# Hybrid encoder block on one core: last block's scans behind the first score tiles, gate steps spread over two heads, weight remainders off GpSimd, heads 4 to 7 first in the out projection

## Chip, cores and metric

The kernel runs on one core of a Trainium2 chip. The metric is the device time of one execution in microseconds (us). The engines are called by the profile's short names: PE (TensorE), DVE (VectorE), ACT (ScalarE), POOL (GpSimd), and SP (SyncE, which here only issues transfers).

## What is computed

One layer of an encoder with two branches beside each other. 1024 tokens and 16 meta tokens of width 1024 are normalized and projected once; the attention branch and the recurrent branch are gated, added, projected and added to the input; a second norm and a SwiGLU network of width 2816 follow, which the change does not touch.

```
proj = rmsnorm(h, norm1_g) @ w_in
q, k, v, xr, gr, g_merge = split(proj)
attn = bidirectional_gqa(rope(rmsnorm(q)), rope(rmsnorm(k)), v)     # 8 heads of 128, 2 key heads
xc   = centred_dwconv(xr)                                           # 4 taps
rnn  = (rg_lru(xc, ..., reverse=False) + rg_lru(xc, ..., reverse=True)) * gelu(gr)
g_attn, g_rnn = split(sigmoid(g_merge))
h = h + (g_attn * attn + g_rnn * rnn) @ w_out
h = h + swiglu(rmsnorm(h, norm2_g))

def rg_lru(xc, wa, ba, wx, bx, lam, reverse):
    r, i = sigmoid(xc @ wa + ba), sigmoid(xc @ wx + bx)             # 8 blocks of 128 channels
    a = exp(8 * r * log_sigmoid(lam))
    u = sqrt(1 - a * a) * (i * xc)
    h[t] = a[t] * h[t - 1] + u[t]                                   # or from the end
```

## The kernel before

A product in single precision is made of three matmuls: each operand is split into a rounded part and a remainder (`split`: ACT writes the rounded part with a Copy, line 100, another engine the remainder with a subtraction, line 102), and `mm3` adds hi·hi, hi·lo and lo·hi. The remainder is made on DVE, or on POOL where `split` is called with `G`.

The program has these stages, by the time of the profiled execution. Up to 488 us: norm and projections, and then a loop over the eight blocks `b` of the recurrent branch. For each block PE makes the products of the gate branch (`gm`, `gr`) and of the block's own gates (`gates`), `decays` makes the decays, and `scans` the square roots (ACT), the two scans and the result (DVE), which is stored as `rm_d[b]`. `tg` is the block's branch for the gelu. Behind the loop the first half of head 0's merge gate is made: the product `ga` on PE, then `gate`: a tanh on ACT (line 640) and one step on POOL. A tile scheduler lays out each engine's order from the order of the code, its priorities and the buffers; ACT has to load a table of functions when the kind of function changes.

From 488 to about 800 us: attention. It loops over heads `h` and over eight tiles `i` of 128 queries. The scores of a tile (27 matmuls into three banks, `S0` or `S1` by turns, `emit_scores`) are followed by the maximum on DVE (`nm`), the exponential on ACT (`p`), a scaled copy on ACT and its remainder on DVE (`PP`, two instructions, of 1024 and 16 columns) and a transposing transfer (`PT`). A scores buffer is free for the next tile but one when `p` is made. After every second tile the pair of tiles that lies two pairs back gets its product with v (`pv`, 25 matmuls, `emit_pv`), which DVE multiplies into the gate (`gar`). Between these, PE gets fill work in steps of 6 matmuls: the gate projection of the head after next (`ga_steps`, product `gap`), and in head 7 the out projection of heads 0 to 3 (`out_steps`, product `oph`, copied by DVE to `h`, line 804). `pv`, `gap` and `oph` share two "fill" banks by turns. How many fill steps follow a tile is set by hand:

```
            for _ in range(1 if h or i > 4 else 2 if i > 1 else 3):
                next(steps, None)
```

During heads 6 and 7 a table `ahead` sets by hand after which tile a load or a split of the out projection's operands stands: `M` (heads 0 to 3, loaded from DRAM; `M[c]` for each half c of the queries), `MH` (heads 4 to 7, head 4 loaded, the others straight from `gar`, function `keep`), and `wo` (eight pieces of the weights, `load_wout`; the remainder on POOL). A name in it means the next of two steps of that piece: load, then split.

From about 770 to 880 us: the rest of the out projection (`ops`, by `out_tile(t, n, kh)`: eight query tiles t, two column halves n, and kh = 0 for heads 0 to 3, that is `M`, kh = 1 for heads 4 to 7, that is `MH`), with the second norm of finished tiles and their transposes (`hT`) beside it. Then the network.

The functions that the change touches, with the line numbers of the profile:

Of the kernel before, what the change touches and what calls it, by code (L numbers as in the profile page):

```python
# [9 lines left out]
F32 = mybir.dt.float32  # L10
# [3 lines left out]
AF = mybir.ActivationFunctionType  # L14
ALU = mybir.AluOpType
# [5 lines left out]
T = 1024  # L21
NM = 16
NK = T + NM
HD = 128
NH = 8
NKV = 2
NB = 8
# [17 lines left out]
def tile_hybrid_encoder_block(  # L45
# [25 lines left out]
    V, S, G, PE, SP = nc.vector, nc.scalar, nc.gpsimd, nc.tensor, nc.sync  # L71
# [133 lines left out]
    def project(name, w, chunks):  # L205

        for c, a, e, o in chunks:
            ps = bank0(name)
            feat_project(ps[:, 0:e - a], w, c, a, e)
            yield ps[:, 0:e - a], o, e - a  # L210
# [305 lines left out]
    def load_gates(b):  # L516
        raw = pb.tile([128, 2, 2, 128], F32, name="graw")
        SP.dma_start(out=raw[:, :, 0], in_=rg_wa[0][:, b].rearrange("r c d -> c r d"))
        SP.dma_start(out=raw[:, :, 1], in_=rg_wx[0][:, b].rearrange("r c d -> c r d"))
        w = pb.tile([128, 2, 2, 2, 128], F32R, name="gw")  # L520
        split(raw, w[:, 0], w[:, 1])
        return w
# [50 lines left out]
                    S.activation(out=p[:, kind, a:e], in_=ps, func=AF.Sigmoid, bias=bias)  # L573
        return ri

    def decays(b, ri, xc):
        aa = page([128, 2, NK], F32, "aa")
        for r in range(2):
            p = ri[r]
            lo = 0 if r == 0 else NM  # L580
            rr, ii = p[:, 0, lo:NK], p[:, 1, lo:NK]
            a1, a2 = aa[:, r, lo:NK], pb.tile([128, NK], F32, name="a2")[:, lo:NK]
            cc = slice(8 * r + b, 8 * r + b + 1)
            S.activation(out=a1, in_=rr, func=AF.Exp, scale=ncL[:, cc])
            S.activation(out=a2, in_=a1, func=AF.Square)
            S.activation(out=rr, in_=rr, func=AF.Tanh, scale=cL[:, cc])

            V.scalar_tensor_tensor(out=rr, in0=a2, scalar=1.0, in1=rr, op0=ALU.add, op1=ALU.mult)
            V.tensor_tensor(out=ii, in0=ii, in1=xc[:, lo:NK], op=ALU.mult)
        return aa  # L590

    def scans(b, ri, aa, tg):
        for r in range(2):
            rr = ri[r][:, 0, (0 if r == 0 else NM):NK]
            S.activation(out=rr, in_=rr, func=AF.Sqrt)
        for r in range(2):
            p = ri[r]
            lo = 0 if r == 0 else NM
            rr, ii, a1 = p[:, 0, lo:NK], p[:, 1, lo:NK], aa[:, r, lo:NK]
            V.tensor_tensor(out=ii, in0=ii, in1=rr, op=ALU.mult)  # L600
            if r:
                rr, ii, a1 = rr[:, ::-1], ii[:, ::-1], a1[:, ::-1]
            V.tensor_tensor_scan(out=rr, data0=a1, data1=ii, initial=0.0, op0=ALU.mult, op1=ALU.add)
        hf, hb = ri[0][:, 0, NM:NK], ri[1][:, 0, NM:NK]
        V.tensor_tensor(out=hf, in0=hf, in1=hb, op=ALU.add)
        V.tensor_tensor(out=hf, in0=hf, in1=tg, op=ALU.mult)
        SP.dma_start(out=rm_d[b], in_=hf)

    def load_head(h, later=None):
# [6 lines left out]
            later.append(lambda: split(raw, q[:, 0], q[:, 1], G))  # L616
        return q

    gw = load_gates(0)
    conv = xr_project(0, xr0)  # L620
    for b in range(NB):
        sg = gm_project(b, next_block())
        tg = pb.tile([128, T], F32, name="tg")
        gr = gr_project(b, next_block(), sg, tg)
        next(gr)
        if b + 1 == NB:
            q = load_head(0)
        ri = gates(b, gw, conv[1])
        w = next_block()
        if b + 1 < NB:  # L630
            gw = load_gates(b + 1)
        next(gr)
        aa = decays(b, ri, conv[0])
        if b + 1 < NB:
            conv = xr_project(b + 1, project("xr", w, ALL))
        scans(b, ri, aa, tg)

    def gate(dst, ps):

        S.activation(out=dst, in_=ps, func=AF.Tanh, scale=0.5)  # L640
        G.tensor_scalar(out=dst, in0=dst, scalar1=1.0, scalar2=undo, op0=ALU.add, op1=ALU.mult)

    ga0 = page([128, 2, T], F32, "gar")
    SP.dma_start(out=ga0[:, 1], in_=rm_d[0])
    w_ga = next_block()

    for ps, o, n in project("ga", w, REAL[:1]):
        gate(ga0[:, 0, o:o + n], ps)

    p1b_pool.__exit__(None, None, None)  # L650
    psp.__exit__(None, None, None)
# [70 lines left out]
    def load_gar(h):  # L722
        g = page([128, 2, T], F32, "gar")
        SP.dma_start(out=g[:, 1], in_=rm_d[h])
        return g
# [19 lines left out]
    def behind():  # L745

        return copies[-3], maxima[-1]
# [26 lines left out]
    wo = {}  # L774

    def load_wout(j, n):

        raw = raw_tile([128, 2, 512])
        SP.dma_start(out=raw, in_=w_out[256 * j:256 * j + 256, 512 * n:512 * n + 512].rearrange("(k p) c -> p k c", p=128))
        wo[j, n] = page([128, 2, 2, 512], F32R, "wo")  # L780
        yield
        split(raw, wo[j, n][:, :, 0], wo[j, n][:, :, 1], G, behind=(copies[-3], None))
        yield


# [23 lines left out]
    def out_steps():  # L809
# [5 lines left out]
                yield from out_half(t, n, 0, fill_bank("oph"))  # L815

    pend = []
    gar = {0: ga0, 1: load_gar(1)}
    steps = chain(ga_steps(w, ga0, [1]), ga_steps(w_ga, gar[1]))

    items = {
        "M0": load_mix(0, 0), "M2": load_mix(0, 2), "M4": load_kept(4), "w00": load_wout(0, 0), "w10": load_wout(1, 0),
# [2 lines left out]
    }  # L825
    ahead = {
        (6, 1): ["M0", (5, 0)],
        (6, 2): ["M2"],
        (6, 3): ["M0", "w00"],
        (6, 4): ["w10"],  # L830
        (6, 5): ["M2", "w00", (5, 1)],
        (6, 6): ["w01"],
        (6, 7): ["w10", "M4"],
        (7, 0): ["w11"],
        (7, 1): ["w01", (6, 0)],
        (7, 3): ["M4", "w11", "w20"],
        (7, 5): [(6, 1)],
        (7, 6): ["w30"],
        (7, 7): ["w20", "w21", "w30", "w31", "w21", "w31"],
    }  # L840
    later = {}

    for h in range(NH):
        for i in range(8):
            emit_scores(h, i, q)
            for fn in later.pop((h, i), ()):
                fn()
            if i == (1 if h < NH - 2 else 0) and h + 1 < NH:
                q_n = load_head(h + 1, later.setdefault((h, i + 2), []))
            if i == 2 and h + 2 < NH:  # L850
                w_ga = load_block(COL_GA + 128 * (h + 2), G, later.setdefault((h, 4), []))
            if i == 3 and h + 2 < NH:
                gar[h + 2] = load_gar(h + 2)
            for nm in ahead.get((h, i), ()):
                if nm in items:
                    next(items[nm])
                else:
                    keep(*nm)
            if i == 5 and h + 2 < NH:
                steps = ga_steps(w_ga, gar[h + 2])  # L860
            if (h, i) == (NH - 1, 0):
                steps = out_steps()
            if i % 2 == 1:
                if len(pend) > 1:
                    u = pend.pop(0)
                    emit_pv(*u, gar[u[0]])
                pend.append((h, i // 2))
            for _ in range(1 if h or i > 4 else 2 if i > 1 else 3):
                next(steps, None)
        q = q_n  # L870
    for _ in steps:
# [48 lines left out]
    def norm2_rows(t):  # L920
        y = t4([128, D], F32, "y2")
        norm_rows(hres[t], 128, g2b, y)
        SP.dma_start(out=h_d[t], in_=hres[t])
        return y
# [68 lines left out]
    def out_tile(t, n, kh):  # L993
        for _ in out_half(t, n, kh, bank("ops")):
            pass
# [6 lines left out]
    for t in range(4):  # L1002
        xr[t] = raw_tile([128, D])
        SP.dma_start(out=xr[t], in_=x[128 * t:128 * t + 128])
        out_tile(t, 1, 1)
        V.tensor_tensor(out=hres[t], in0=hres[t], in1=xr[t], op=ALU.add)
        ys[t] = norm2_rows(t)
    for t in range(4, 8):
        out_tile(t, 0, 0)

# [146 lines left out]

    ww = {}  # L1160
    for t in range(4):
        out_tile(4 + t, 1, 0)
        norm2_lower(t, ys.pop(t))
        if t < 3:
            ww[4 + t] = wholes(4 + t)
# [5 lines left out]

    for t in range(4, 8):
        for n in range(2):
            out_tile(t, n, 1)
        ys[t] = norm2_rows(t)
        if t == 4:
            step_prep(0, 3)
        else:
            if t > 5:
                up(t - 2)  # L1180
            if t < 7:
                prep_early(t - 4)
# [170 lines left out]
```

## Time and profile before

| | |
|---|---|
| time of three runs | 1497.53, 1498.09, 1499.05 us; median 1498.09 |
| profiled execution | 1500.6 us, of which its span (first to last instruction) is 1498.7 us |
| mean granted clock of PE over the span | 0.995 of full speed |
| PE | busy 1472.1 us, 98% of the span, 7323 matmuls |
| DVE, ACT, POOL | busy 1116.7 us (75%), 744.6 us (50%), 249.2 us (17%) |

Times in the rows of a profile are counted from the start of the span. A row of the timeline gives start, length, engine, line, operation, output and inputs, and in brackets how long the engine had stood idle before it and what it waited for. An "x2" at the end means that neighbouring instructions of the same kind are drawn together, their lengths added.

### The profile page before, as it was taken

Reading aid. Unit: us, or ns where it says so; the run is one execution under the profiler, and the core shown is the slowest. Engines: PE = TensorE matmul, PEld = TensorE weight load, DVE = VectorE, ACT = ScalarE, POOL = GpSimd, SP = SyncE. Lnnn points to the kernel's source line nnn. Section 1 sums busy time; section 2 is a strip of 40 time slices with the busy share of each in tenths; the row PEclk is TensorE's granted clock in tenths of the full one; section 3 lists DMA queues with packets and bytes.
Section 4 is the critical chain, followed back from the end, with each engine's and each line's share of the span. In section 5 each row is a group of like instructions: output and inputs, shape, how many; then the busy total and the mean of one; then the engine's idle time right before and its main releaser. Section 6 shows DMA issues by size and latency. Waiting matters only on the chain. (4 is left out here: it accounts for less than half of the span.)

```text
span 1498.7 us, 20058 instructions
## 1 busy us (share of the span) xinstructions
PE 1472.1 (98%) x7323; PEld 1237.9 (83%) x7323; DVE 1116.7 (75%) x1707; ACT 744.6 (50%) x1244; POOL 249.2 (17%) x189
## 2 busy tenths in 40 slices
PE   7999999999999899999999999999999999999999
PEld 5888888888888788888877888888888888888887
DVE  6877666666776777777875799988888888747562
ACT  5544476667667666667752362322333332554330
POOL 0000000000000332222330201353433333200000
PEclk9999999999999999999999999999999999999999
DMA  7123212222212479896885334565564443898641
GB/s 247 53 73 101 85 35 64 64 64 63 64 57 71 131 190 206 200 202 159 191 187 185 96 100 140 161 189 191 181 199 161 162 160 115 290 333 282 218 144 59
DMA packets 300737, 219.98 MB, mean 147 GB/s; under 512 B 150648, under 2 KB 244304, under 8 KB 300640
## 3 DMA queue, kind: packets, MB, share of 16 engines
q1 hardware_dynamic: 300640, 218.72, 49.2%
q8 instruction: 57, 0.93, 0.3%
q14 instruction: 40, 0.33, 0.1%
HBM read 131.90 MB, written 51.12 MB: 122 GB/s over the span
## 5 line engine op out<-in xcount | busy, mean ns | idle before, releaser
L100 ACT ACTIVATE pw<-pr 128x1024 fp32r<-128x1024 f32 x77 | 80.3, 1062 | 105.6 <-PE po L1269 68.5
L100 ACT ACTIVATE wS<-s 128x512 fp32r<-128x512 f32 x88 | 53.3, 629 | 134.2 <-DVE s L1055 47.5
L1267 PE MATMUL po<-pw 128*128 128x512 f32 x308 | 119.8, 389 | 0.0
L1268 PE MATMUL po<-pw 128*128 128x512 f32 x308 | 119.8, 389 | 0.0
L1269 PE MATMUL po<-pw 128*128 128x512 f32 x308 | 119.8, 389 | 0.0
L102 DVE TENSOR_TENSOR pw<-pr,pw 128x1024 fp32r<-128x1024 f32 x77 | 92.5, 1241 | 34.9 <-ACT pw L100 28.7
L696 DVE SCALAR_TENSOR_TENSOR PP<-p,pr,PP 128x1024 f16<-128x1024 f32 (+1 forms) x128 | 106.6, 889 | 14.2 <-ACT PP L693 13.9
L687 ACT ACTIVATE p<-S,nm 128x1044 f32<-128x1044 f32 x64 | 72.4, 1131 | 65.5 <-DVE nm L684 55.2
L710 PE MATMUL pv<-PT,vt 128*128 128x256 f16 x800 | 94.6, 276 | 3.0 <-DVE h L804 3.0
L710 PEld LDWEIGHTS <-vt 128*128 128x128 f16 x800 | 76.5, 99 | 16.4 <-issue 3.6
L684 DVE TENSOR_REDUCE nm<-S 128x1 f32<-128x1044 f32 x64 | 78.2, 1236 | 9.2 <-PE S L109 9.0
L693 ACT ACTIVATE PP<-p,pr 128x1040 f16<-128x1040 f32 x64 | 73.9, 1154 | 5.3 <-issue 2.1
L102 DVE TENSOR_TENSOR wS<-s,wS 128x512 fp32r<-128x512 f32 x88 | 70.1, 815 | 0.0
L1267 PEld LDWEIGHTS po<-pw 128*128 128x128 f32 x308 | 57.8, 188 | 12.1
L1269 PEld LDWEIGHTS po<-pw 128*128 128x128 f32 x308 | 57.8, 188 | 12.0
L1268 PEld LDWEIGHTS po<-pw 128*128 128x128 f32 x308 | 57.8, 188 | 11.9
L1130 POOL TENSOR_TENSOR as<-act 128x512 f32<-128x512 f32 x11 | 16.6, 1508 | 305.4 <-DVE act L1118 254.1
L107 PE MATMUL S<-kT,qh 128*128 128x348 f32 (+1 forms) x192 | 62.3, 324 | 2.9 <-ACT p L687 2.9
L108 PE MATMUL S<-kT,qh 128*128 128x348 f32 (+1 forms) x192 | 62.0, 323 | 0.0
L109 PE MATMUL S<-kT,qh 128*128 128x348 f32 (+1 forms) x192 | 62.0, 323 | 0.0
L108 PE MATMUL xr<-xn,wblk 128*128 128x264 f32 (+1 forms) x192 | 61.4, 320 | 0.0
L109 PE MATMUL xr<-xn,wblk 128*128 128x264 f32 (+1 forms) x192 | 61.4, 320 | 0.0
(324 smaller groups left out, 4391.1 us busy)
## 6 DMA issues: line engine op xcount, KB each, us to landing
raw<-in_w_in_dram SPq DMA_DIRECT2D x44, 512.0 KB, 4.2
pr<-act_d SPq DMA_DIRECT2D x77, 256.0 KB, 5.2
raw<-in_w_ffn_in_dram SPq DMA_DIRECT2D x25, 512.0 KB, 4.7
wraw<-in_w_ffn_in_dram SPq DMA_DIRECT2D x22, 512.0 KB, 5.4
raw<-in_w_ffn_out_dram SPq DMA_DIRECT2D x22, 512.0 KB, 4.6
act_d<-as SPq DMA_DIRECT2D x44, 256.0 KB, 2.0
wot_d<-bs SPq DMA_DIRECT2D x44, 256.0 KB, 2.0
pr<-wot_d SPq DMA_DIRECT2D x44, 256.0 KB, 5.3
```

Source lines behind the costliest of these rows:

```text
L100: S.activation(out=hi, in_=src, func=AF.Copy)
L102: return (eng or V).tensor_tensor(out=lo, in0=src, in1=f32(hi), op=ALU.subtract)
L108: PE.matmul(out=ps, lhsT=lh, rhs=rl, start=False, stop=False)
L109: PE.matmul(out=ps, lhsT=ll, rhs=rh, start=False, stop=(k == n - 1))
L684: maxima.append(V.tensor_reduce(out=nm, in_=s[:, :, 0:KC], axis=AX.XY, op=ALU.max, negate=True))
L687: S.activation(out=p, in_=s[:, :, 0:KC], func=AF.Exp, bias=nm, accum_out=den)
L693: S.activation(out=pair[:, 0:NK], in_=pf, func=AF.Copy, scale=r)
L696: V.scalar_tensor_tensor(out=pair[:, o:o + e - a], in0=pf[:, a:e], scalar=r, in1=pair[:, a:e], op0=ALU.mult, op1=ALU.subtract)
L710: PE.matmul(out=ps, lhsT=vt[:, j, hl, vs], rhs=pt[:, m], start=(n == 0), stop=(n == len(terms) - 1))
L1267: PE.matmul(out=banks[t], lhsT=lh, rhs=w[:, 0, 1], start=j == 0, stop=False)
L1268: PE.matmul(out=banks[t], lhsT=lh, rhs=w[:, 1, 1], start=False, stop=False)
L1269: PE.matmul(out=banks[t], lhsT=ll, rhs=w[:, 0, 1], start=False, stop=j == NFP - 1)
```

## The change

Four things are changed. First, the last block's `scans` are taken out of the loop and called in attention behind the second score tile, with `tg` in a buffer of the raw ring, since the block's own buffers are gone by then; the roots get a function of their own, `roots`, and in the last block they are put behind the tanh of `ga`, which now belongs to the loop. Second, a set `rest` names four tiles in heads 5 to 7 that get no fill step, so that head 7's gate steps reach further into head 6, and `out_steps` starts one tile later. Third, the remainders of `wo` go from POOL to DVE, and the table `ahead` is written anew. Fourth, behind attention the products of heads 4 to 7 (kh = 1) come before those of heads 0 to 3 (kh = 0). PE makes the same matmuls, and ACT loads as many tables.

```diff
-    def scans(b, ri, aa, tg):
+    def roots(ri, behind=None):
         for r in range(2):
             rr = ri[r][:, 0, (0 if r == 0 else NM):NK]
-            S.activation(out=rr, in_=rr, func=AF.Sqrt)
+            with tc.issue_after(behind.ins) if behind else nullcontext():
+                S.activation(out=rr, in_=rr, func=AF.Sqrt)
+
+    def scans(b, ri, aa, tg):
...
-        tg = pb.tile([128, T], F32, name="tg")
+        tg = pb.tile([128, T], F32, name="tg") if b + 1 < NB else raw_tile([128, T])
...
+        th = None
+        if b + 1 == NB:
+            ga0 = page([128, 2, T], F32, "gar")
+            SP.dma_start(out=ga0[:, 1], in_=rm_d[0])
+            for ps, o, n in project("ga", w, REAL[:1]):
+                th = gate(ga0[:, 0, o:o + n], ps)
         if b + 1 < NB:
             conv = xr_project(b + 1, project("xr", w, ALL))
-        scans(b, ri, aa, tg)
+        roots(ri, th)
+        if b + 1 < NB:
+            scans(b, ri, aa, tg)
...
-        split(raw, wo[j, n][:, :, 0], wo[j, n][:, :, 1], G, behind=(copies[-3], None))
+        split(raw, wo[j, n][:, :, 0], wo[j, n][:, :, 1], behind=behind())
...
     ahead = {
         (6, 1): ["M0", (5, 0)],
...
+        (7, 5): ["w11", "w20"],
         (7, 6): ["w30"],
-        (7, 7): ["w20", "w21", "w30", "w31", "w21", "w31"],
+        (7, 7): ["M4", (5, 1), "w20", (6, 0), "w30", "w21", (6, 1), "w31", "w21", "w31"],
     }
+    rest = {(5, 6), (6, 0), (6, 2), (7, 0)}
...
+            if (h, i) == (0, 1):
+                scans(NB - 1, ri, aa, tg)
+                gar[1] = load_gar(1)
...
-            if (h, i) == (NH - 1, 0):
+            if (h, i) == (NH - 1, 1):
                 steps = out_steps()
...
-            for _ in range(1 if h or i > 4 else 2 if i > 1 else 3):
+            for _ in range(0 if (h, i) in rest else 1 if h or i > 4 else 2 if i > 1 else 3):
...
     for t in range(4, 8):
-        out_tile(t, 0, 0)
+        out_tile(t, 0, 1)
...
-        out_tile(4 + t, 1, 0)
+        out_tile(4 + t, 1, 1)
...
         for n in range(2):
-            out_tile(t, n, 1)
+            out_tile(t, n, 0)
```

On ACT, at the end of the last block (`ri` are the block's gates, `aa` and `a` its decays, `gar<-ga` the tanh of head 0's first gate half, which frees its bank), before:

```order
L584 ACT_TABLE_LOAD
L584 ACTIVATE aa<-ri,ncL 128x1024
L554 ACTIVATE tg<-tg 128x512
L585 ACTIVATE a_4381<-aa 128x1024
L586 ACTIVATE ri<-ri,cL 128x1024
L595 ACT_TABLE_LOAD
L595 ACTIVATE ri<-ri 128x1040
L595 ACTIVATE ri<-ri 128x1024
L640 ACT_TABLE_LOAD
L640 ACTIVATE gar<-ga 128x512
```

And the same place now (`raw` is now the name of `tg`):

```order
L585 ACTIVATE ri<-ri,cL 128x1040
L554 ACTIVATE raw<-raw 128x512
L583 ACT_TABLE_LOAD
L583 ACTIVATE aa<-ri,ncL 128x1024
L622 ACTIVATE gar<-ga 128x512
L584 ACTIVATE a_4381<-aa 128x1024
L585 ACTIVATE ri<-ri,cL 128x1024
L594 ACT_TABLE_LOAD
L594 ACTIVATE ri<-ri 128x1040
L594 ACTIVATE ri<-ri 128x1024
```

The tanh of `ga` has moved from behind the two roots to the place right behind the second exponential, ahead of a Square, a tanh, a table load and the roots.

On DVE, at the same time in the program (line 600 are the products ahead of the scans, 603 the scans, 605 and 606 the sum and the block's result, `nm` the maxima of the first score tiles), before:

```order
L600 TENSOR_TENSOR ri<-ri 128x1040
L600 TENSOR_TENSOR ri<-ri 128x1024
L603 SCALAR_TENSOR_TENSOR ri<-aa,ri 128x1040
L603 SCALAR_TENSOR_TENSOR ri<-aa,ri 128x1024
L605 TENSOR_TENSOR ri<-ri 128x1024
L606 TENSOR_TENSOR ri<-ri,tg 128x1024
L684 TENSOR_REDUCE nm<-S_4433 128x1
L689 TENSOR_SCALAR den<-den 128x1
L690 RECIPROCAL pr<-den 128x1
L696 SCALAR_TENSOR_TENSOR PP_4435<-p,pr,PP_4435 128x1024
```

And now:

```order
L604 SCALAR_TENSOR_TENSOR ri<-aa,ri 128x1040
L692 TENSOR_REDUCE nm<-S_4427 128x1
L697 TENSOR_SCALAR den<-den 128x1
L604 SCALAR_TENSOR_TENSOR ri<-aa,ri 128x1024
L698 RECIPROCAL pr<-den 128x1
L606 TENSOR_TENSOR ri<-ri 128x1024
L697 TENSOR_SCALAR den<-den 128x1
L607 TENSOR_TENSOR ri<-ri,raw 128x1024
L704 SCALAR_TENSOR_TENSOR PP_4428<-p,pr,PP_4428 128x1024
L704 SCALAR_TENSOR_TENSOR PP_4428<-p,pr,PP_4428 128x16
L698 RECIPROCAL pr<-den 128x1
L692 TENSOR_REDUCE nm<-S_4426 128x1
```

The maximum of the first tile stands ahead of this piece now, that of the second between the two scans, and the third tile's maximum comes behind the scans, the result and the first tile's PP.

On DVE, in the last pair of score tiles (tiles 6 and 7 of head 7; the product `gar<-gar,pv` frees a fill bank, COPY h<-oph another), before:

```order
L684 TENSOR_REDUCE nm<-S_4433 128x1
L684 TENSOR_REDUCE nm<-S_4434 128x1
L689 TENSOR_SCALAR den<-den 128x1
L690 RECIPROCAL pr<-den 128x1
L712 TENSOR_TENSOR gar<-gar,pv 128x256
L689 TENSOR_SCALAR den<-den 128x1
L690 RECIPROCAL pr<-den 128x1
L696 SCALAR_TENSOR_TENSOR PP_4437<-p,pr,PP_4437 128x1024
```

And now:

```order
L692 TENSOR_REDUCE nm<-S_4427 128x1
L102 TENSOR_TENSOR MH<-raw,MH 128x1024
L697 TENSOR_SCALAR den<-den 128x1
L102 TENSOR_TENSOR MH<-gar,MH 128x512
L698 RECIPROCAL pr<-den 128x1
L102 TENSOR_TENSOR wo<-raw,wo 128x2x512
L697 TENSOR_SCALAR den<-den 128x1
L720 TENSOR_TENSOR gar<-gar,pv 128x256
L704 SCALAR_TENSOR_TENSOR PP_4430<-p,pr,PP_4430 128x1024
L704 SCALAR_TENSOR_TENSOR PP_4430<-p,pr,PP_4430 128x16
L698 RECIPROCAL pr<-den 128x1
L102 TENSOR_TENSOR MH<-gar,MH 128x512
```

Two remainders of `MH` and one of `wo` now stand between the second maximum and the product that frees the bank, and more behind it; all eight remainders of `wo` stand on DVE from tile 7 of head 6 on.

## Rows read from the trace of the kernel before

**Rows 1.** The page: span, engine totals, and the exponential's group (busy, mean ns).

```profile
span 1498.7 us, 20058 instructions
...
PE 1472.1 (98%) x7323; PEld 1237.9 (83%) x7323; DVE 1116.7 (75%) x1707; ACT 744.6 (50%) x1244; POOL 249.2 (17%) x189
...
L687 ACT ACTIVATE p<-S,nm 128x1044 f32<-128x1044 f32 x64 | 72.4, 1131 | 65.5 <-DVE nm L684 55.2
```

**Rows 2.** Waits of PE by who ended them: total, times, longest.

```profile
PE gap L735 <- ACT gar L640: 4.4, 1, 4.4
PE pv L710 <- DVE h L804: 3.0, 1, 3.0
PE S L107 <- ACT p L687: 2.9, 1, 2.9
PE ops L800 <- DVE M L102: 2.5, 1, 2.5
...
PE xT L282 <- DVE ne L139: 0.6, 1, 0.6
```

**Rows 3.** Windows: length, busy PE, PEld, DVE, ACT, POOL, then granted clock, DMA.

```profile
18.00:26.00 8.00, 7.39 (x37) 5.90 (x36) 6.84 (x15) 5.25 (x12) 0.00 (x0) 1.00 1.03 408
...
487.00:500.50 13.50, 9.13 (x36) 6.87 (x34) 11.51 (x9) 7.90 (x9) 4.28 (x1) 0.87 0.09 23
724.00:738.00 14.00, 11.07 (x67) 9.90 (x65) 11.96 (x19) 9.69 (x16) 5.85 (x5) 0.88 0.78 194
762.00:772.00 10.00, 7.01 (x40) 5.45 (x40) 7.97 (x10) 7.44 (x11) 7.12 (x4) 0.83 0.80 185
811.00:823.00 12.00, 9.54 (x40) 7.47 (x39) 9.37 (x14) 3.09 (x7) 0.00 (x0) 0.86 0.59 186
```

**Rows 4.** Timeline of ACT at the end of the last block.

```profile
485.45 1.15 ACT L584 ACTIVATE aa<-ri,ncL 128x1024 f32<-128x1024 f32 x1
...
487.02 1.05 ACT L585 ACTIVATE a<-aa 128x1024 f32<-128x1024 f32 x1
...
493.75 0.60 ACT L640 ACTIVATE gar<-ga 128x512 f32<-128x512 f32 x1
```

**Rows 5.** Timeline of DVE, start of attention: the scans and the block's result.

```profile
493.82 4.50 DVE L603 TENSOR_TENSOR_SCAN ri<-aa,ri 128x1040 f32<-128x1040 f32 x2
...
499.84 1.23 DVE L606 TENSOR_TENSOR ri<-ri,tg 128x1024 f32<-128x1024 f32 x1
```

**Rows 6.** Timeline of PE: first matmuls of score tiles, a fill, the last wait.

```profile
514.72 0.32 PE L107 MATMUL S<-kT,qh 128*128 128x348 f32 x1
...
742.91 0.32 PE L107 MATMUL S<-kT,qh 128*128 128x348 f32 x1
...
744.33 0.48 PE L798 MATMUL oph<-wo,M 128*128 128x512 f32 x1
...
745.81 0.32 PE L107 MATMUL S<-kT,qh 128*128 128x348 f32 x1
...
751.37 0.32 PE L107 MATMUL S<-kT,qh 128*128 128x348 f32 x1
...
817.53 0.50 PE L800 MATMUL ops<-wo,M 128*128 128x512 f32 x1 [2.46 <-DVE M L102]
```

**Rows 7.** Timeline of DVE, head 7 and the out projection.

```profile
745.61 2.77 DVE L696 SCALAR_TENSOR_TENSOR PP<-p,pr,PP 128x1024 f16<-128x1024 f32 x4
...
756.90 2.39 DVE L684 TENSOR_REDUCE nm<-S 128x1 f32<-128x1044 f32 x2
...
761.69 4.98 DVE L696 SCALAR_TENSOR_TENSOR PP<-p,pr,PP 128x1024 f16<-128x1024 f32 x4 [0.50 <-ACT PP L693]
766.60 0.68 DVE L804 COPY h<-oph 128x512 f32<-128x512 f32 x1
...
816.25 2.36 DVE L102 TENSOR_TENSOR M<-raw,M 128x1024 fp32r<-128x1024 f32 x2
```

**Rows 8.** Timeline of POOL, end of head 7.

```profile
764.14 7.11 POOL L102 TENSOR_TENSOR wo<-raw,wo 128x1024 fp32r<-128x1024 f32 x3 [2.14 <-ACT wo L100]
```

More of the change, by code (lines that the diff above doesn't have):

```diff
@@ L574, in gates, with decays @@
         return ri
-    def decays(b, ri, xc):
-        aa = page([128, 2, NK], F32, "aa")
+    def decays(b, ri, aa, xc):
         for r in range(2):
@@ L589, in decays @@
             V.tensor_tensor(out=ii, in0=ii, in1=xc[:, lo:NK], op=ALU.mult)
-        return aa
-    def scans(b, ri, aa, tg):
+    def roots(ri, behind=None):
         for r in range(2):
             rr = ri[r][:, 0, (0 if r == 0 else NM):NK]
-            S.activation(out=rr, in_=rr, func=AF.Sqrt)
+            with tc.issue_after(behind.ins) if behind else nullcontext():
+                S.activation(out=rr, in_=rr, func=AF.Sqrt)
+    def scans(b, ri, aa, tg):
         for r in range(2):
@@ L617, in load_head, with gate @@
         return q
+    def gate(dst, ps):
+        th = S.activation(out=dst, in_=ps, func=AF.Tanh, scale=0.5)
+        G.tensor_scalar(out=dst, in0=dst, scalar1=1.0, scalar2=undo, op0=ALU.add, op1=ALU.mult)
+        return th
     gw = load_gates(0)
@@ L632, in tile_hybrid_encoder_block @@
         next(gr)
-        aa = decays(b, ri, conv[0])
+        aa = page([128, 2, NK], F32, "aa")
+        decays(b, ri, aa, conv[0])
+        th = None
[4 more added lines that the diff above has]
+                th = gate(ga0[:, 0, o:o + n], ps)
         if b + 1 < NB:
             conv = xr_project(b + 1, project("xr", w, ALL))
-        scans(b, ri, aa, tg)
[L638 to L644, printed above, removed]
+        roots(ri, th)
+        if b + 1 < NB:
+            scans(b, ri, aa, tg)
     w_ga = next_block()
-    for ps, o, n in project("ga", w, REAL[:1]):
-        gate(ga0[:, 0, o:o + n], ps)
     p1b_pool.__exit__(None, None, None)
@@ L817, in tile_hybrid_encoder_block, with second_gate @@
     pend = []
-    gar = {0: ga0, 1: load_gar(1)}
-    steps = chain(ga_steps(w, ga0, [1]), ga_steps(w_ga, gar[1]))
+    gar = {0: ga0}
+    def second_gate():
+        yield from ga_steps(w_ga, gar[1])
+    steps = chain(ga_steps(w, ga0, [1]), second_gate())
     items = {
@@ L827, in tile_hybrid_encoder_block @@
         (6, 1): ["M0", (5, 0)],
[L828 to L837, printed above, removed]
+        (6, 3): ["M0", "M2"],
+        (6, 5): ["M2", "w00"],
+        (6, 6): ["w10"],
+        (6, 7): ["w00", "w01"],
+        (7, 1): ["w10", "w11"],
+        (7, 3): ["w01", "M4"],
+        (7, 5): ["w11", "w20"],
         (7, 6): ["w30"],
-        (7, 7): ["w20", "w21", "w30", "w31", "w21", "w31"],
+        (7, 7): ["M4", (5, 1), "w20", (6, 0), "w30", "w21", (6, 1), "w31", "w21", "w31"],
     }
+    rest = {(5, 6), (6, 0), (6, 2), (7, 0)}
     later = {}
```

## The prediction

> **What bounds the kernel now.** I read the page first: the span is 1498.7 us and TensorE (PE) is busy for 1472.1 of it, 98% [rows 1]. The change alters no matmul, so it can only move time that PE spends waiting, or time at a lower clock. The waits of PE say where that is: behind the first loads, which the change doesn't touch, four waits stand out, 4.4, 3.0, 2.9 and 2.5, and the others are like the 0.6 shown with them [rows 2]. The windows around the four show the second half of their price: in each the mean granted clock is down, 0.87, 0.88, 0.83 and 0.86, because after the wait PE runs on the lower level (1.2 GHz) for some 3.4 us before it is back on 2.4 GHz [rows 3]. I count for each place the idle time plus (1 − clock) times the window:
>
> - A, start of attention: 4.37 + 0.13 × 13.5 = 6.1
> - B, before the score tiles of head 7: 2.93 + 0.12 × 14.0 = 4.6
> - C, end of head 7: 2.99 + 0.17 × 10.0 = 4.7
> - D, out projection: 2.46 + 0.14 × 12.0 = 4.1
>
> Together 19.5 us are all that this change can win, and 1498.1 − 19.5 = 1478.6 is the floor. The profiled execution took 1500.6, 0.17% above the median of the runs, and its span is 1.9 less; differences worked out inside the span I take off the median, 1498.1.
>
> **A, the scans.** PE's first gate step waits for a bank that ScalarE's tanh of `ga` frees, and this tanh runs at 493.75, behind a Square at 487.02, a tanh, two table loads and two roots [rows 4]. It ends at 494.35, so PE, which waited 4.4, got there at about 490.0 [rows 2, 4]. In the changed order the tanh stands right behind the exponential that ended at 485.45 + 1.15 = 486.60 before [rows 4]; a Square and a tanh of 1040 columns (about 1.1 each) and a tanh of 512 (0.6) now stand ahead of that exponential, so it ends near 489.4 and the tanh of `ga` near 490.0. The wait becomes 0 to 0.3: taken as 0.
>
> What is late next: the Square, the roots, and so the scans start 3.1 later (490.1 for 487.02). On VectorE (DVE) the chain of products, scans and the last multiplication ended at 499.84 + 1.23 = 501.07 [rows 5]; now it ends at 504.2, and with the second tile's maximum (1.2) between the scans at 505.4. Behind it stand PP of the first tile (1.4), two small steps (0.3) and the maximum of the third tile (1.2), to 508.3; its exponential takes 1.13 [rows 1], to 509.4. The fifth tile's scores need that buffer. PE started them at 514.72 [rows 6] and would come 6.1 sooner, at 508.6. So a new wait appears, 0.8 by this sum; if GpSimd, whose gate step took place beside the scans, makes these DVE steps some tenths slower it is up to 2.3. I take 1.2. A gains 6.1 − 1.2 = 4.9. On SP's queue the store of the eighth block's result and the loads of three gate rows now stand ahead of the first transposes; the store is ready at about 505, before the first PP (506.8), so it holds up none. The gate tile `tg` takes one of the three raw buffers until the scans end, so the first head's q is loaded some blocks' steps later, but still in the eighth block, with its split done before 488: cost 0, its cover being the block's own gate and projection steps.
>
> **B and C, head 6 to head 7.** Both come from DVE falling behind; at C the bank that PE's pv waits for comes free with the copy at 766.60, right behind four PP instructions. The four PP of a pair of tiles take 2.77 at 745.61, but 4.98 at 761.69, where GpSimd works on three `wo` remainders in 7.11 at 764.14 [rows 7, 8]: 2.2 more, while the split of the same size on DVE costs 2.36 / 2 = 1.18 [rows 7]. So a remainder costs DVE 1.0 less if DVE does it itself, where the two would overlap; where they wouldn't, it costs 1.2 more. The Trainium skill, "Perfetto Trace Analysis", Optimizing Scalar/DVE Operations, advises to take work off a saturated DVE, and warns that between DVE and GpSimd, which share a port, this might not help. The advice speaks against this change, the warning for it; by the advice alone eight remainders would only add 8 × 1.2 to DVE and the time would go towards that of the slower rival below.
>
> The second half is the gate steps. A pair of score tiles with two fills takes PE 751.37 − 742.91 = 8.46; one fill is 745.81 − 744.33 = 1.48, so with one 6.98, with none 5.50 [rows 6]. Before, three tiles had none between head 6 and 7; now four pairs have one each and the others two. DVE's time for a pair: from the maxima to PP 761.69 − 756.90 = 4.79 with a small split in it, plus 2.77, is 7.6 [rows 7]; a split of 1024 columns in the place of the small one makes it 7.7 to 7.8, a copy of an `oph` bank (0.68) besides 8.3 to 8.4. So DVE loses 0.6 to 1.1 in each pair with one fill, and regains up to 0.7 in one with two. I walked through the changed order from 692 with these times. The maxima of the pairs start on DVE at 710.1 (tile 2 of head 6), 718.2, 725.9, 733.7 (tile 0 of head 7), 741.4 and 749.7, the first tile's exponential ends 2.4 later (1.23 + 1.13), and PE wants the buffer at 713.0, 721.4, 729.7, 736.6, 744.9 and 753.3. It has 0.6, 0.8, 1.4, 0.5, 1.1 and 1.2 to spare: no wait at B.
>
> At the end it runs out. In the last pair DVE now does two MH splits and a `wo` split before the product that frees a `pv` bank: the second maximum ends at 760.9, then 1.2 + 0.7 + 1.2 + 0.4 and small steps, to 764.4, where PE wants the bank for an out-projection step at 763.0: 1.4. The step after next needs the copy of the bank before, behind two PP pairs and three more splits, 0.8 late. So of B and C, 9.3, I expect 2.2 to come back: gain 7.1.
>
> **Price of the new waits.** Does the clock drop after a wait of 0.8 to 1.4? No row here has one of that length. The wait of 0.6 near the start left the clock at 1.00 [rows 2, 3]; that of 2.46 was followed by 0.86 × 12 us [rows 3]. Both ends stay for the range: 0 or 1.7 for each. I take 0, as 1.2 and 1.4 are nearer to 0.6.
>
> **D, the order of the out projection.** PE waited until 817.53 for M of the second half, whose two splits (816.25, 2.36) stand on DVE behind norm2's work [rows 7]. Of the 108 matmuls of heads 4 to 7, whose inputs have long been split, the changed order puts all ahead of it, where before 48 were; the 60 more take 60 × 1.48 / 6 = 14.8 [rows 6], so M is wanted at 817.53 − 2.46 + 14.8 = 829.9 at the earliest, and even at their present place the splits end at 816.25 + 2.36 = 818.6. The cover is 11 us; without it the old wait would be back. Norm2's chain for the transposes between these products stays where it is on DVE and ScalarE. Gain 4.1.
>
> **Sum.** 4.9 + 7.1 + 4.1 = 16.1, and 1498.1 − 16.1 = **1482.0 us**.
>
> **The rivals.**
> - *DVE runs out sooner at the end.* A pair that costs DVE 0.2 more than worked out (the splits may take longer beside the products on GpSimd) adds 1.4 at the end: the wait of 1.4 becomes 2.8, over the 2.46 that did bring the lower clock, so 1.4 + 1.7 on top: 1485.
> - *The scans hold up the first tiles.* With DVE 1.3 later than worked out the wait at the fifth tile is 2.5 and the clock drops: 1.3 + 1.7 on top, again 1485. Both together give 1488.
> - *The stalls only move.* DVE's total work isn't less, and PE has no slack of its own: waits of the old size come back in other pairs. Then 1498. Against it: with GpSimd quiet there DVE's own pairs shrink by 2.2 where it collided, and the gate steps do fill the gaps.
> - *Slower: DVE becomes the bound.* From tile 7 of head 6 on eight remainders are added to DVE; PE's windows show it busy for 11.96 of 14 us just there [rows 3]. This decides if a remainder costs over 1.18 + 16.1/8 = 3.2 us each; at 3.8 it gives 1498 + 5 = 1503. The Trainium skill's page named above has the rule for it. Nothing on DVE of that shape takes over 1.2 while GpSimd is quiet.
> - *No new wait at all*: 1478.6.
>
> **How the numbers follow.** Chances: forecast 0.48 (own range 1480 to 1484); end sooner 0.18; first tiles 0.12; both 0.07; no new wait 0.06; stalls only move 0.05; slower 0.04. The range 1478 to 1489, from the floor to a little over both mishaps together, holds these but the last two, 0.91 by this count; I keep it that wide because the price of the clock drop rests on two rows. A measurement can tell 0.2%, 3 us. Faster 0.91, same 0.05, slower 0.04.
>
> **What would show it.** In the waits of PE the four of before should be gone: none on `gap` by the tanh of `ga`, none on `ops` by M; in their place one on S by `p` near 508 and one or two on `oph` near 763, each 0.7 to 1.5. The four PP of a pair should stay near 2.8 to head 7's end, and 128x1024 `wo` splits on DVE near 1.2. I am wrong if a wait of over 2 us stands anywhere behind 480, or if the granted clock drops in a place that had none.

## The result

| | before | after |
|---|---|---|
| median of the timed runs | 1497.81 us (1497.34 to 1499.05, 4 runs) | 1487.9 us (1487.38 to 1488.4, 4 runs) |
| ratio after / before, 95% interval | | 0.993 (0.9918 to 0.9942) |
| span of the profiled execution | 1498.7 us | 1486.6 us |
| mean granted clock over the span | 0.995 | 0.999 |

The change makes the kernel faster by 0.7%, 9.9 us of the forecast 16.1; the time lies in the range (1478 to 1489), near its upper end. The page after, span and engines:

```profile
span 1486.6 us, 20069 instructions
...
PE 1466.1 (99%) x7323; PEld 1233.6 (83%) x7323; DVE 1114.4 (75%) x1715; ACT 744.6 (50%) x1244; POOL 225.8 (15%) x181
```

The waits of PE after, by who ended them (total, times, longest), where [rows 2] had 4.4, 3.0, 2.9 and 2.5:

```profile
PE S L107 <- ACT p L695: 2.4, 1, 2.4
PE oph L806 <- DVE gar L720: 1.5, 1, 1.5
PE oph L806 <- DVE h L812: 0.9, 1, 0.9
PE gap L743 <- ACT gar L622: 0.6, 1, 0.6
...
PE pv L718 <- DMA PT<-PP: 0.4, 1, 0.4
```

All four old waits are gone or short, and the new ones stand where the forecast put them: one on S by `p`, two on `oph` by the `gar` product and by the copy. The two at the end have the size forecast (1.5 and 0.9 for 1.4 and 0.8); that on S has twice its size, 2.4 for 1.2, and there are two small ones, 0.6 and 0.4, that I had put at nothing. The windows of [rows 3] after, and one more around the new wait (length, busy PE, PEld, DVE, ACT, POOL, granted clock, DMA):

```profile
487.00:500.50 13.50, 12.90 (x62) 10.41 (x61) 10.67 (x11) 11.60 (x14) 2.32 (x6) 1.00 0.11 36
505.00:520.00 15.00, 12.59 (x63) 10.88 (x62) 12.79 (x18) 10.06 (x15) 5.81 (x5) 0.89 0.81 215
724.00:738.00 14.00, 14.00 (x98) 12.32 (x97) 12.57 (x22) 10.24 (x16) 2.32 (x3) 1.00 0.87 200
762.00:772.00 10.00, 7.66 (x32) 5.68 (x32) 10.00 (x16) 6.09 (x10) 1.72 (x1) 1.00 0.82 187
811.00:823.00 12.00, 12.00 (x63) 10.12 (x62) 10.29 (x19) 5.18 (x10) 1.29 (x1) 1.00 0.80 255
```

The clock is at 1.00 in all four old places, with waits of 1.5 and 0.9 in the fourth row; only around the wait of 2.4 it is down, 0.89. The timeline of DVE after shows why that wait is so long; the row of POOL under it stands beside the first:

```profile
502.62 1.23 DVE L606 TENSOR_TENSOR ri<-ri 128x1024 f32<-128x1024 f32 x1
...
503.88 3.42 DVE L607 TENSOR_TENSOR ri<-ri,raw 128x1024 f32<-128x1024 f32 x1
507.23 1.42 DVE L704 SCALAR_TENSOR_TENSOR PP<-p,pr,PP 128x1024 f16<-128x1024 f32 x2
...
508.65 1.22 DVE L692 TENSOR_REDUCE nm<-S 128x1 f32<-128x1044 f32 x1
...
503.82 2.41 POOL L102 TENSOR_TENSOR qh<-raw,qh 128x1024 fp32r<-128x1024 f32 x1 [4.13 <-ACT qh L100]
```

The last step of the scans takes 3.42 where it took 1.23 [rows 5], while GpSimd makes the remainder of head 1's q for 2.41. That pushes the maximum of the third tile from the forecast 507.1 to 508.7, and PE stands still until its exponential is done. In the trace of before the same remainder ran at 501.03, beside one maximum and a DVE that stood idle behind it (DVE, then POOL):

```profile
500.98 1.24 DVE L684 TENSOR_REDUCE nm<-S 128x1 f32<-128x1044 f32 x1
...
501.03 2.40 POOL L102 TENSOR_TENSOR qh<-raw,qh 128x1024 fp32r<-128x1024 f32 x1 [2.29 <-ACT qh L100]
```

At the other end of attention the forecast's steps can be read one by one from DVE's timeline:

```profile
727.54 1.22 DVE L102 TENSOR_TENSOR wo<-raw,wo 128x1024 fp32r<-128x1024 f32 x1
...
754.90 2.89 DVE L704 SCALAR_TENSOR_TENSOR PP<-p,pr,PP 128x1024 f16<-128x1024 f32 x4 [0.50 <-ACT PP L701]
...
762.48 1.20 DVE L102 TENSOR_TENSOR wo<-raw,wo 128x1024 fp32r<-128x1024 f32 x1
763.60 0.14 DVE L697 TENSOR_SCALAR den<-den 128x1 f32<-128x1 f32 x1
763.67 0.40 DVE L720 TENSOR_TENSOR gar<-gar,pv 128x256 f32<-128x256 f32 x1
```

A remainder of `wo` takes 1.2 on DVE, the four PP of a pair 2.9 where they took 4.98 [rows 7], and the product that frees the bank ends at 764.1 (forecast 764.4).

### The profile page after: what moved, and what is told of

It reads as the page before. It is cut to its first block, busy times and chain, and to the rows that moved or that the text cites. A ratio compares the mean times of both kernels' runs of the same rounds, so it can differ in the third digit from the quotient of the medians.

```text
span 1486.6 us, 20069 instructions
## 1 busy us (share of the span) xinstructions
PE 1466.1 (99%) x7323; PEld 1233.6 (83%) x7323; DVE 1114.4 (75%) x1715; ACT 744.6 (50%) x1244; POOL 225.8 (15%) x181
## 4 chain that ended last, share of the span: by engine, by line
PE 48%; DVE 3%; issue 1%; ACT 1%; ACTq 0%; DVEq 0%
PE po L1285 5%; PE po L1284 5%; PE po L1283 5%; PE A11B L1085 1%; PE A11B L1086 1%; PE A12B L1085 1%; PE S3T L1085 1%; PE S4B L1085 1%; PE A22T L1085 1%; PE S1T L1085 1%; PE S2T L1085 1%; PE S4B L1086 1%; PE A22T L1086 1%; PE S1T L1086 1%; PE S2T L1086 1%; PE S3T L1086 1%
## 5 line engine op out<-in xcount | busy, mean ns | idle before, releaser
L704 DVE SCALAR_TENSOR_TENSOR PP<-p,pr,PP 128x1024 f16<-128x1024 f32 (+1 forms) x128 | 98.2, 824 | 14.1 <-ACT PP L701 14.1
L1284 PEld LDWEIGHTS po<-pw 128*128 128x128 f32 x308 | 57.8, 188 | 12.1
```

The lines of the kernel that those rows point to most:

```text
L704: V.scalar_tensor_tensor(out=pair[:, o:o + e - a], in0=pf[:, a:e], scalar=r, in1=pair[:, a:e], op0=ALU.mult, op1=ALU.subtract)
L1284: PE.matmul(out=banks[t], lhsT=lh, rhs=w[:, 1, 1], start=False, stop=False)
```

## The experiments

My theory after the result: B and C went as forecast; the missing 6 us are the collision at the first tiles with what follows from it, and a profiled execution of before that had more clock drops than most. The rivals: the scans' chain is too long by itself, or another part of the change brought less than I think. The kernel before, timed beside these runs, has medians of 1497.8 to 1499.1, so a difference of about 1 us between two kernels that were not timed side by side says little.

### What each part is worth

**The scans where they were.** The changed kernel with the scans and the tanh of `ga` back at the end of the last block:

```diff
-        tg = pb.tile([128, T], F32, name="tg") if b + 1 < NB else raw_tile([128, T])
+        tg = pb.tile([128, T], F32, name="tg")
...
-            if (h, i) == (0, 1):
-                scans(NB - 1, ri, aa, tg)
```

> The changed kernel without its first part: the scans stand at the end of the last block again, tanh of ga behind the roots. Theory: the old wait of 4.4 with its clock drop (6.1 together) comes back, but the new ones (0.6, 2.42 with a drop of 1.65, 0.4, together 5.1) go: 1487.9 + 1.0 = 1489, so the first part bought about 1. Rival (the first part bought the 4.9 that was forecast and the loss is elsewhere): 1492.8.

Measured: 1489.66 us (1489.31 to 1489.74), ratio to before 0.9941 (0.9928 to 0.9953). The first part of the change is worth 1489.66 − 1487.9 = 1.8 by these times; against the kernel before as it was timed beside each, 1498.65 here and 1497.81 with the changed kernel, the two are 9.0 and 9.9 less, which makes it 0.9. Neither is near 4.9. The waits of PE in this run: the old one is back, and S and PT have none over 0.2.

```profile
PE gap L735 <- ACT gar L640: 4.4, 1, 4.4
PE oph L798 <- DVE gar L712: 1.5, 1, 1.5
PE oph L798 <- DVE h L804: 0.9, 1, 0.9
```

**The remainders of `wo` on GpSimd again.**

```diff
-        split(raw, wo[j, n][:, :, 0], wo[j, n][:, :, 1], behind=behind())
+        split(raw, wo[j, n][:, :, 0], wo[j, n][:, :, 1], G, behind=(copies[-3], None))
```

> The changed kernel with the eight remainders of wo on GpSimd again, everything else as changed. Theory (collisions on DVE decide): PP x4 of the pairs from tile 7 of head 6 take 4 to 5 in place of 2.8, DVE falls behind by 1 per pair, and PE waits 2 to 3 at the end of head 7 or before, with a clock drop: 1490 to 1493. Rival (spreading the gate steps did it, the place of the remainders is the same either way): 1488.

Measured: 1496.18 us (1494.47 to 1498.12), 8.3 slower than the changed kernel, more than the theory's 2 to 5. The rows of DVE and POOL show the collision:

```profile
737.73 4.97 DVE L704 SCALAR_TENSOR_TENSOR PP<-p,pr,PP 128x1024 f16<-128x1024 f32 x4 [0.50 <-ACT PP L701]
...
748.01 5.09 DVE L704 SCALAR_TENSOR_TENSOR PP<-p,pr,PP 128x1024 f16<-128x1024 f32 x4 [0.38 <-ACT PP L701]
...
740.18 2.50 POOL L102 TENSOR_TENSOR wo<-raw,wo 128x1024 fp32r<-128x1024 f32 x1 [2.13 <-ACT wo L100]
...
750.46 2.62 POOL L102 TENSOR_TENSOR wo<-raw,wo 128x1024 fp32r<-128x1024 f32 x1 [2.01 <-ACT wo L100]
```

Each remainder beside PP makes the four of them 5.0 instead of 2.8, and PE gets three waits of 1.7, 1.8 and 2.4 on `oph`. Behind the wait of 2.4, near 769, the clock falls (0.86 over 764 to 776). This profiled execution is the fastest of the ten, 1.7 under their median; where the others lose that is not seen in it. In all ten the time is 2.3 to 2.6 over the span, where the executions of the other kernels have 1.7 to 1.9, so some 0.7 of the 8.3 lies outside the first to the last instruction; why stays open.

**The remainders of `wo` on DVE, and nothing else,** the same line in the kernel before:

> The kernel before with the eight remainders of wo on DVE and nothing else (table, gate steps, scans and out projection as before). Theory (the collisions of PP with GpSimd made both waits in heads 6 and 7): the wait of 2.93 near 730 falls under 1.5 and that of 2.98 near 764 under 2, both without a clock drop, the time falls by 5 to 8: 1490.5 to 1493.5. Rival (the missing fill made the wait near 730, and more work on DVE makes the one near 764): both stay at 2 or more, 1496 to 1499.

Measured: 1492.06 us (1490.78 to 1493.06) beside 1498.86 for before, 6.8 less. In its trace no wait over 0.7 is left in heads 6 and 7; the two that [rows 2] show there are gone, though three tiles still have no fill. So the collisions made both waits, and the gate steps' rival falls. (With the remainder on DVE the same line also puts it behind the last maximum; that order wasn't tried apart from the engine.) The waits left there are 0.3 + 0.5 + 0.6 + 0.6 = 1.9 in sum, no more than the 2.35 that the whole change leaves: in these heads the traces show no gain from the gate steps and the new table on top of the remainders.

```profile
PE gap L735 <- ACT gar L640: 4.4, 1, 4.4
PE ops L800 <- DVE M L102: 1.8, 1, 1.8
PE kvps L294 <- ACT xn L100: 0.7, 1, 0.7
```

**The gate steps as before,** in the changed kernel:

```diff
-    rest = {(5, 6), (6, 0), (6, 2), (7, 0)}
+    rest = set()
...
-            if (h, i) == (NH - 1, 1):
+            if (h, i) == (NH - 1, 0):
                 steps = out_steps()
```

> The changed kernel with the gate steps as before (no tile without one in heads 5 to 7, out projection from the first tile of head 7), remainders on DVE. Theory: the three tiles without fill come back and PE waits there, but less than before since DVE's PP are short now: 1 to 2 at head 6 to 7, perhaps with a clock drop: 1489 to 1491. Rival (the collisions alone made that wait): 1488; rival (the missing fill alone made it): a wait of 2.9 with a drop, 1492.5.

Measured: 1489.99 us (1489.57 to 1490.33), 2.1 slower, as expected (1.2, if each is taken against the kernel before timed beside it): the waits near 730 to 740 are 0.6, 0.7 and 0.6, and the clock stays at 1.00. By the waits, spreading the steps is worth 2.0 there less 0.9, by which the waits at the end of head 7 are shorter here, so about 1.1; as much again is a longer wait on PT near 526 (1.5 for 0.4), far from where the steps were moved. This holds beside the new table `ahead`; with the old one, in the run above, the steps weren't needed.

**The order of the out projection alone,** in the kernel before:

```diff
     for t in range(4, 8):
-        out_tile(t, 0, 0)
+        out_tile(t, 0, 1)
...
-        out_tile(4 + t, 1, 0)
+        out_tile(4 + t, 1, 1)
...
-            out_tile(t, n, 1)
+            out_tile(t, n, 0)
```

> The kernel before with the fourth part alone: the products of heads 4 to 7 first in the out projection. Theory: the wait of 2.46 for M goes, with its clock drop where there is one: 2.5 to 4.1 less than before, 1494.5 to 1496.1, and no wait over 0.7 between 800 and 880. Rival (norm2's rows come late for the transposes once M isn't waited for): a wait of 1 or more on hT, 1497 to 1498.

Measured: 1495.25 us (1494.52 to 1495.9) beside 1498.63, ratio 0.9979 (0.9969 to 0.9988): 3.4 less, and no wait left in that stage.

### The kernel before, traced twice more

> The kernel before once more, for a second trace of it. Theory (the forecast's sum was too large because the profiled execution of before carried a clock drop after each of its four waits, and others don't): the four waits are 4.4, 2.9, 3.0 and 2.5 within 0.2, but at least one of the four windows has a granted clock of 0.97 or more; span 1495.5 to 1497.5. Rival: all four drops are there, and the span is near 1498.5 as before.

> The same kernel a third time, with the same expectations: by the theory one drop or more missing, and not always after the same wait; by the rival all four there.

Measured: 1498.5 and 1496.67 us, spans 1496.6 and 1494.8. The first two waits are as in [rows 2]; that at the end of head 7 is 2.96 and 2.62 for 2.98, and the fourth 1.9 and 1.7 for 2.5. Windows of the first look, then, in a second fence, of the second; the granted clock is the third number from the end:

```profile
487.00:500.50 13.50, 9.13 (x36) 6.84 (x34) 11.45 (x9) 7.90 (x9) 4.28 (x1) 0.87 0.08 22
...
762.00:772.00 10.00, 7.04 (x40) 5.56 (x39) 7.98 (x10) 7.44 (x11) 7.19 (x4) 0.83 0.86 206
811.00:823.00 12.00, 10.08 (x49) 8.10 (x48) 10.14 (x17) 3.89 (x8) 0.00 (x0) 1.00 0.64 205
```

```profile
487.00:500.50 13.50, 9.13 (x32) 6.91 (x30) 11.66 (x10) 7.69 (x8) 4.41 (x2) 0.75 0.13 40
...
762.00:772.00 10.00, 7.38 (x49) 6.35 (x48) 8.66 (x13) 7.42 (x12) 7.86 (x4) 1.00 0.81 194
811.00:823.00 12.00, 10.31 (x50) 8.31 (x49) 10.19 (x19) 3.68 (x9) 0.00 (x0) 1.00 0.79 254
```

In both the last window keeps its clock, 1.00 where [rows 3] have 0.86; in the second look the third does too, and the first is at 0.75. The theory holds for the clock; that all four waits come back within 0.2 doesn't, and the second span is 0.7 under the one expected. What a wait costs in clock differs from one execution to the next, and the one that the forecast was made from had the dearest out projection of the three.

### The new wait at the first tiles

**Head 1's q split held back,** so that GpSimd is quiet during the scans' last step:

```diff
-            later.append(lambda: split(raw, q[:, 0], q[:, 1], G))
+            later.append(lambda: split(raw, q[:, 0], q[:, 1], G, behind=(copies[-1] if h == 1 else None, None)))
```

> The changed kernel, with the split of head 1's q held back until ACT has copied the fourth tile, so that GpSimd's remainder (2.41 us) no longer runs beside the last step of the scans. Theory (collision): that step, which took 3.42 us beside GpSimd, goes back to 1.2; the maximum of the third tile ends 2.2 sooner; PE's wait at the fifth tile shrinks from 2.42 to at most 0.5 and the clock stays up: 1487.9 - 2.0 - 1.7 = about 1484.2. Rival (the chain of scans itself is too long): the wait keeps 1.5 or more, with the clock drop, 1486.5 to 1488.

Measured: 1487.62 us (1487.13 to 1487.89). The mechanism is as the theory has it, the time is not. The step is back at 1.21, and PE no longer waits on S; but it waits on the transposes instead, 1.5 and 1.2. The remainder that was held back now meets PP, 4.88 for 2.8, and that of the gate weights stands beside two maxima. The clock stays at 1.00, so by waits and clock this run should be 1.4 under the changed kernel; the times have 0.3 (1.1, each taken against the kernel before timed beside it). Its waits of PE have a row for PT, and the timeline below it shows DVE, then POOL:

```profile
PE pv L718 <- DMA PT<-PP: 2.8, 2, 1.5
```

```profile
505.41 1.21 DVE L607 TENSOR_TENSOR ri<-ri,raw 128x1024 f32<-128x1024 f32 x1
...
513.02 4.88 DVE L704 SCALAR_TENSOR_TENSOR PP<-p,pr,PP 128x1024 f16<-128x1024 f32 x4 [0.70 <-ACT PP L701]
517.82 2.38 DVE L692 TENSOR_REDUCE nm<-S 128x1 f32<-128x1044 f32 x2
...
515.47 2.39 POOL L102 TENSOR_TENSOR qh<-raw,qh 128x1024 fp32r<-128x1024 f32 x1 [7.22 <-ACT qh L100]
517.81 2.36 POOL L102 TENSOR_TENSOR wblk<-raw,wblk 128x1024 fp32r<-128x1024 f32 x1
```

**The transfers ahead of the second transpose moved too.** The store of the last block's result goes behind the sixth tile's transpose, and every later head's q is loaded behind the transpose that was issued last:

```diff
+            if (h, i) == (0, 5):
+                with tc.issue_after(turns[-1].ins):
+                    SP.dma_start(out=rm_d[NB - 1], in_=hf7)
...
-        SP.dma_start(out=raw, in_=q_d[h])
+        with tc.issue_after(turns[-1].ins) if h > 1 else nullcontext():
+            SP.dma_start(out=raw, in_=q_d[h])
```

> The changed kernel with the split of head 1's q held back (as in the run that did it alone) and, further, the store of the last block's result and the loads of the next heads' q behind the first transposes on SP. Theory (after the collision the transposes are late, because a store and a load of 512 KB each stand ahead of the second one): the two waits of pv on PT, 1.5 and 1.2, go or shrink to 0.5, and the time falls by 2 to 2.7 from 1487.6: 1485 to 1485.6. Rival (the transposes are late because the PP instructions before them are, beside GpSimd's other remainders): the waits on PT stay and so does the time, 1487.5.

Measured: 1496.85 us (1496.35 to 1498.26), 9 slower than the changed kernel: a miss of both. The first wait on PT does go, but the loads of gate weights now stand right behind the held-back loads of q (582.67 in this trace, for a remainder that GpSimd makes at 590.56, 584.75 with q late alone), and PE waits for them in later heads (three waits on `wblk`, 2.5 together). Besides there are 3.2 on the gate's tanh, ending at 520.8, with 3.4 of clock behind it, 1.95 on PT, ending at 723.9, with 1.7 of clock, and 1.6 on a remainder of `wo`.

**Only the store, and head 2's q** (the condition in the last lines is `h == 2`, and `turns[1]`, the second tile's transpose):

> The kernel with head 1's q split held back, and on SP only the store of the last block's result (behind the sixth tile's transpose) and the load of head 2's q (behind the second tile's) moved; all other loads where they were. Theory (store and load ahead of the second transpose make the first pv wait): the second transpose lands some 2 sooner, the wait of 1.5 on PT near 515 goes, and no wait on wblk comes, as the ring of raw buffers isn't held up: about 1486, 1.5 under 1487.6. Rival (any transfer moved off there comes back as a late load or a late later transpose): other waits of the same sum, 1487 to 1488 or more.

Measured: 1489.03 us (1488.76 to 1489.35), 1.1 slower. The second transpose, issued at 509.4 here and at 509.5 with q late alone, takes 1.70 for 4.93, so store and load had made it late. No wait on PT or S is left; in their place stands one of 3.1 on the gate's tanh, which ACT now makes behind the exponential of the fifth tile, and that is late since PP took 4.87. The clock after it is down to 0.76. PE's waits, and the window (columns as above):

```profile
PE gap L748 <- ACT gar L627: 3.7, 2, 3.1
```

```profile
513.00:527.00 14.00, 10.86 (x55) 9.40 (x54) 11.75 (x16) 8.53 (x14) 6.11 (x4) 0.76 1.00 243
```

**GpSimd's two remainders taken apart,** on top of that: gate weights behind the fourth tile's copies, head 1's q behind the sixth's:

```diff
-                q_n = load_head(h + 1, later.setdefault((h, i + 2), []))
+                q_n = load_head(h + 1, later.setdefault((h, i + (2 if h else 4)), []))
...
-            later.append(lambda: split(raw, w[:, 0], w[:, 1], eng))
+            later.append(lambda: split(raw, w[:, 0], w[:, 1], eng, behind=(copies[3] if len(copies) == 5 else None, None)))
```

> As the run with the store and head 2's q moved on SP, but with GpSimd's two remainders taken apart: the split of head 2's gate weights stands behind the fourth tile's copies on ACT, that of head 1's q only behind the sixth tile's. Theory (each of GpSimd's 2.4 us remainders lengthens the DVE steps that it meets, and what is late next follows from that alone): no wait on S or PT near 508 to 515, and the wait of 3.1 on the gate's tanh near 517 goes, since that tanh now stands ahead of the fifth tile's exponential on ACT; what is left is 0.6 near 489 and 1.5 and 0.9 at the end: about 1484 to 1485. Rival (the first tiles have no room at all once the scans stand among them): waits of 2 or more in sum stay between 505 and 550, 1486.5 or more.

Measured: 1488.38 us (1487.5 to 1489.09), the same as the changed kernel within 0.1%. By its sign the rival holds: three waits on S (1.3, 1.2 and 0.7) have taken the place of the one. Two pairs' PP are long now instead of one, each beside one remainder. PE's wait on S, and the timeline of DVE, then POOL:

```profile
PE S L107 <- ACT p L700: 3.2, 3, 1.3
```

```profile
512.86 4.87 DVE L709 SCALAR_TENSOR_TENSOR PP<-p,pr,PP 128x1024 f16<-128x1024 f32 x4 [0.70 <-ACT PP L706]
...
522.43 5.16 DVE L709 SCALAR_TENSOR_TENSOR PP<-p,pr,PP 128x1024 f16<-128x1024 f32 x4 [0.38 <-ACT PP L706]
...
515.31 2.39 POOL L102 TENSOR_TENSOR wblk<-raw,wblk 128x1024 fp32r<-128x1024 f32 x1 [7.22 <-ACT wblk L100]
...
524.88 2.68 POOL L102 TENSOR_TENSOR qh<-raw,qh 128x1024 fp32r<-128x1024 f32 x1 [1.95 <-ACT qh L100]
```

Put beside each other, PE's waits between 505 and 550 come to 2.42 + 0.39 = 2.8 in the changed kernel, 1.54 + 1.21 + 0.30 = 3.1 with q late, 3.1 with the store late, 3.2 + 0.2 = 3.4 with the remainders apart; the clock behind them costs 1.7, 0, 3.4 and 0 in these traces. The waits of about 3 us move, and keep their size. From 497 to 510 DVE's timeline shows it idle for no more than 0.2 at a time, in the changed kernel as with q late, and each remainder that GpSimd makes adds some 2.2 to the TENSOR_TENSOR or PP that it meets. That the waits had to come back for this reason is argued, not shown: a version with all of these remainders beside maxima was not run. No version run here beats the changed kernel by more than 0.1%.

## Why the forecast held, and where it failed

The time lies in the stated range, but not in the forecast's own (1480 to 1484), and both signs of being wrong that the prediction named came true: a wait of over 2 us behind 480, 2.42, and a clock drop where there had been none, at 511. Of the 6 us that are missing, A makes 4.9 − 1.1 = 3.8 and the baseline 19.5 − 17.3 = 2.2. The range had been drawn for two mishaps, one at the first tiles and one at the end of attention. The first happened; the second didn't, and it is luck that the room left for it covered the baseline.

| part | forecast gain | by the traces and runs |
|---|---|---|
| A, scans behind the first tiles | 4.9 | 1.1 by the waits and clock of the traces, 0.9 to 1.8 by the run without it |
| B and C, head 6 to head 7 | 7.1 | 7.0 by the traces; 6.8 for the remainders alone |
| D, out projection | 4.1 | 1.7 to 1.9 in two of three executions of before; 3.4 by the run of it alone |

- **A, the old wait: right.** The tanh of `ga` ran at 489.60 and ended at 490.2 (forecast 490.0), and the bound of 0.3 was exceeded by little, a wait of 0.6.
- **A, the new wait: the term that was mis-sized.** I took 1.2 from a range of 0.8 to 2.3 and thought of GpSimd's gate step as the only neighbour. The neighbour was the remainder of head 1's q, which I had not placed on GpSimd's queue at that time, although B and C of the same forecast were built on just this collision. It cost 3.42 − 1.21 = 2.2 on DVE. The wait was 2.42, and with it came the clock drop that I had priced at nothing, 0.11 × 15 = 1.65 in the profiled execution. With 0.6 and 0.39 of small waits A gave back 5.1 of 6.1. The run with q late shows that this neighbour made the wait on S, and also that taking it away doesn't bring the 4.9: the transposes are late then, a second term that I had put at nothing (the store on SP "holds up none"). Store and load ahead of it make the second transpose 4.93 long, for 1.70 without them, and PE waits 1.5. The rival on the first tiles, wait of 2.5 with a drop, had a chance of 0.12 and is what happened; its time, 1485, was still too low because of the next point.
- **The baseline: the second step that failed.** The sum was made inside one profiled execution (1500.6) and taken off a median of 1498.1. The 2.5 between them were part of the very waits that I took away: by the first of the other two traces the four places cost 4.37 + 2.93 + 2.96 + 1.92 = 12.2 of waiting and 1.8 + 1.7 + 1.7 of clock, 17.3 and not 19.5. The places after cost 5.8 and 1.65, 7.4. The difference is 9.9, and the spans differ by 1496.6 − 1486.6 = 10.0. With the profiled execution of the forecast it is 12.1 for 12.1, with the third trace 9.3 for 8.2. The runs agree with the first of these: 9.9.
- **B and C: right in size, and in the half of the mechanism that is the remainders.** No wait near 730, remainders at 1.2, PP at 2.8 to 3.2, and 1.46 + 0.89 = 2.35 at the end for 2.2. The maxima that the forecast walked through, 710.1 to 749.7, ran at 708.7 to 749.4. (What DVE loses in a pair with one fill is 0.6 to 0.8 by the forecast's own terms, not up to 1.1.) The other half, the gate steps, wasn't needed beside the old table: the remainders alone took both old waits away. That DVE would become the bound with eight remainders more did not happen: to have them on GpSimd costs 6.8 in the kernel before and 8.3 in the changed one. The Trainium skill, "Perfetto Trace Analysis", Optimizing Scalar/DVE Operations, advises to take work off a saturated DVE, and warns that this might not help between DVE and GpSimd, which share a port. The warning is borne out here: PP takes 5.0 beside a remainder on GpSimd, for 2.8.
- **D: right in kind,** the wait is gone in every run with it and no transpose became late; the size was that of the dearest of three executions. Such executions aren't rare: of the 21 of before that were timed beside the run of it alone, nine have a mean clock of 0.995, as the forecast's had, and ten one of 0.997.

## What to carry to other kernels

When work is moved under an engine's queue, list what the neighbour that slows it down will do in the same microseconds, not only what it did there before; the remainder that hurt here had run beside a maximum and an idle DVE. Where an engine has no idle time, putting off a single item may only move the wait to the next consumer, as in the three orders that were tried here on top of the changed kernel without holding up later heads. And make the sum against an execution at the median, or look at a second trace, when the waits to be removed carry a cost that comes and goes.

## What the hardware showed that I had not expected

- The clock drop behind a wait is not settled by the wait's length. A wait of 2.4 at the same place, before the fifth tile's scores, was followed by 0.89 over 15 us in the changed kernel and by 1.00 in the two runs with the remainders back on GpSimd and with the gate steps as before; one of 2.39 in the first of these two, near 769, was followed by 0.86 over 12 us. One of 2.6 (second look at before) left 1.00, one of 3.0 (first look) 0.83. Waits of 4.4 at one place gave 0.87 and 0.75 over 13.5 us, and one of 3.1 gave 0.76 over 14 us: 0, about 1.7 or about 3.4 us each. A wait of 1.95 (the run with every q load held back) was followed by 0.88 over 14 us, one of 1.92 (first look) by 1.00, and behind 480 us none shorter by a drop. What decides between them was not settled.
- DVE's maxima don't mind GpSimd. The two of a pair took 2.38 beside a whole remainder of 2.36 on GpSimd (the rows of the run with q late, at 517.8), while a TENSOR_TENSOR or PP beside one takes some 2.2 more. The Trainium skill, "SBUF — State Buffer", Who interferes with whom, says that a DVE instruction with two inputs in SBUF (the memory on the chip that the engines work from) contends with a GpSimd instruction that reads there, and that one with at most one such input doesn't, outside the modes that use both ports. The traces agree: TENSOR_TENSOR and PP have two such inputs, a maximum reads only the scores. A place under the maxima would then be free for these remainders; no run here tried to put them all there.
